# Silu by Tanh and root reciprocals by Newton steps on GpSimd, and the products of a slice ordered by columns, in a two-block fp32 transformer kernel

## The chip, the cores and the metric

The kernel runs on one core of one Trainium2 chip. The metric is the device time of one execution in microseconds (us). The time of a kernel is the median of several executions. Engines are called as in the profile: PE is TensorE's matmul, PEld its weight load, DVE is VectorE, ACT is ScalarE, POOL is GpSimd, SP is SyncE, which issues the weight loads from HBM.

## The reference

Two blocks follow each other on 256 tokens of width 2048, batch 1, all in float32.

The first block has two layers. Each layer modulates a root-mean-square norm (`x * rsqrt(mean(x^2) + 1e-6)`) with a shift and a scale that come from `silu(c) @ w_mod`, multiplies by `w_in` (2048 x 8192), and sends the result through a gated short convolution (`silu(z) * rmsnorm(b * conv(c * h))`) and through a bidirectional retention of 8 heads, whose output is normalised per head and multiplied by `silu(z)`. Both halves go through `w_out` (2048 x 2048), times a gate, into the residual. In layer 0 a context of 256 tokens takes the same way, so that 512 columns are worked on; layer 1 needs only keys and values of it.

The second block is a mixer with a state-space branch (causal convolution of width 4 with a bias and `silu`, a chunked scan, a gate `silu(z)`, a norm per group) and a dilated window attention branch with softmax, over `w_in_2` (2048 x 12320) and `w_out_2` (4096 x 2048), and then a squared-ReLU feed-forward net (2048 to 8192 to 2048). Each of the two is followed by a norm and added to the residual.

The new arithmetic rests on two identities: `silu(z) = (tanh(z/2) + 1) * z/2`, and Newton's step for `y = 1/sqrt(x)`, which is `y <- y * (1.5 - 0.5 * x * y * y)`.

## The kernel before

All products are float32 products on PE in the format fp32r, each made of three: an operand `w` is split into `wh` (what fp32r keeps) and `wl = w - wh`, the other operand likewise, and `wh*ah + wh*al + wl*ah` is summed in PSUM. Weights come from HBM through five buffers `raw` of 128 x 1024, by SP's queue. For each buffer ACT writes `wh` (an `ACTIVATE` of 128 x 1024, line L163) and DVE writes `wl` (a `TENSOR_TENSOR` of the same size, L166).

The program is written out in one order by a planner. `chunk` (from line 215) appends *jobs*. One job is one buffer of weights, usually two slices of 128 rows of the matrix (`kts`, a slice of k) for four column groups of 128 or one of 512. `run` (from line 365) goes through the jobs; for each it first emits the conversions of jobs up to four ahead (`AHEAD`), as far as a pair of `wh`/`wl` slots is free: three pairs always, and more where `room` lends a region of the activation arena `ar` to a stretch of jobs as `extra` slots. Then it emits the job's matmuls bank by bank (there are up to four PSUM banks `pm` to a job). After each bank comes an `event` (line 318): it emits what was put off by `later`, by one event or by `lag` of them. Once per job it takes a `step` (line 342) of the first *side*, a generator that holds the work beside the matmuls: `ret` (retention, one per two heads), `conv_fin`, `norms2`, `ssd`, `att`, `h2n_side`. A side whose `later` pieces are still waiting doesn't step. Every engine runs its own instructions in the order in which they were emitted, so a small matmul of a side stands between the big ones on PE, and PE waits there if its input is late.

Two kinds of products matter here. With `mmA` and `mmB` (lines 281 and 305) all matmuls of a bank have the same number of columns, 512 or 256. With `mmW` (line 288) a slice of k gives two matmuls: `wh` against 512 columns (`ah` and `al` side by side) and `wl` against the 256 columns of `ah`, added into the second half of the bank. In a job of two slices a bank's order is therefore 512, 256, 512, 256 columns, and the next bank goes on the same way. `mmW` serves the convolution columns of layer 1, the second half of layer 1's output product, most of the mixer's input product, the second half of its output product, and the feed-forward net's first product but for its first 1024 columns.

Norms are taken in one form, `rms_cols` (line 541): DVE scales the mean square and adds epsilon (L171), ACT takes `Sqrt` in place, DVE the `RECIPROCAL` (L544), on tiles of 128 x 2 or 128 x 4. Then PE spreads the column over the partitions (`spread`, line 557, four or eight small matmuls), and the normalising instructions read that. It is called once at the start (`prep_x`), twice in `norm1` (the context's and the tokens' norm ahead of layer 1), in `conv_fin` of both layers, twice in a row in `norms2`, in `norm3` and in `h2n_side`. `ret` (16 times), `ssd` (8 times) and the tail (`sums_out`, `scale_out`, twice) have their own `Sqrt`, put off by three events in `ret` and `ssd`, and `RECIPROCAL` (L852, L1462, L1846). `sqrt_table` makes ACT load the table of `Sqrt` ahead of `norm1` and `norm3`.

`Silu` is an `ACTIVATE` in six places: on `c` in `prelude`, on z in `evac_qz`, `conv_evac`, `conv_evac1` and `evac_z`, and after the convolution in `taps2`. `Exp` is used in `ret`, `ssd`, `att` and `dt_side`. A change between `Silu`, `Sqrt` and `Exp` puts an `ACT_TABLE_LOAD` in ACT's queue.

The feed-forward net starts right behind `norm3`: `h2_kt` (line 711) makes one slice of its input per job, with a chain of DVE (L174), POOL (L1715, a `TENSOR_TENSOR` add of 128 x 256), ACT and DVE. From the sixth job of this stretch on `room(u0 + 6, ...)` (line 1811) lends two more slots.

The tail: the last product's four banks are added (L166), squared and summed on ACT, multiplied by a weight on POOL (L1826); `sums_out`, `scale_out` and `store_out` (lines 1834 to 1854) scale 128 x 512 pieces on DVE (L174) and store them.

Of the kernel before, what the change touches and what calls it, by code (L numbers as in the profile page):

```python
# [10 lines left out]
OP = mybir.AluOpType  # L11
# [90 lines left out]
class Prog:  # L102
# [112 lines left out]
    def chunk(self, W, N, pieces, n, groups, items, mm, evac, pre=None, need=None, ord_=None, merge=False, fine=False, dense=False):  # L215
# [11 lines left out]
        for gi, kts in enumerate(groups):  # L227
            def pe(hi, lo, gi=gi, kts=kts):
# [8 lines left out]
                for bi, b in enumerate(order):  # L237
                    bank = st["banks"][b]
                    seq = [(h[:, ki], l[:, ki], kt) for h, l, ks in parts for ki, kt in enumerate(ks)]
                    for si, (h, l, kt) in enumerate(seq):  # L240
                        for ii, it in enumerate(items[b]):
                            todo = mm(it, kt, h, l)
                            for pi, (x, y, *at) in enumerate(todo):
                                o, n = at or (it["o"], it["n"])
                                self.mm(bank[:, o:o + n], x, y, start=gi == 0 and si == 0 and ii == 0 and pi == 0,
                                        stop=last and si == len(seq) - 1 and ii == len(items[b]) - 1 and pi == len(todo) - 1)
                        if (nb == 2 and si % 2 == 0 and len(kts) == 2) or (dense and last and si < len(seq) - 1):
                            self.event()
                    self.event((lambda: evac(b, bank)) if last else None)
                    for _ in range(places.count(bi)):  # L250
                        yield
# [196 lines left out]
    def startup(self):  # L448
# [15 lines left out]
        self.b1 = self.small(32)  # L464

# [9 lines left out]
    def prelude(self):  # L475
# [5 lines left out]
        self.act(self.csil, self.cv("c", 0, 32).rearrange("p (v k) -> p v k", v=2), AF.Silu)  # L481
# [3 lines left out]
        for l in range(2):  # L485
            self.ts(self.b1[:, l * 16:(l + 1) * 16], self.cv("b_mod", l * 48 + 16, 16), 1.0, op0=OP.add)
        self.spawn(self.prep_x())
# [53 lines left out]
    def rms_cols(self, out, ms, k):  # L541
        self.ts(out, ms, k, EPS, OP.mult, OP.add)
        self.act(out, out, AF.Sqrt)
        self.nc.vector.reciprocal(out, out)  # L544
# [8 lines left out]

    def sqrt_table(self):
        self.act(self.tcol, self.ones[:, 0:1], AF.Sqrt)
# [195 lines left out]
    def evac_qz(self, t, bank):  # L751
        self.act(self.R["q"][:, t], bank[:, 0:256])
        self.act(self.R["z"][:, t], bank[:, 256:512], AF.Silu)
        if t < 2:
            self.later(lambda: self.rope(self.R["q"][:, t], t))
# [20 lines left out]
    def ret(self, l, g):  # L776
# [6 lines left out]
        for hh in range(2):  # L783
# [64 lines left out]
            self.later(lambda: self.act(sd, sd, AF.Sqrt), lag=3)  # L848
            yield

            def normed():
                self.nc.vector.reciprocal(sd, sd)  # L852
# [15 lines left out]
    def conv_evac(self, l, fts):  # L868
# [14 lines left out]
        def evac(b, bank):  # L883
# [6 lines left out]
            elif b == 3:  # L890
                self.act(Z, bank, AF.Silu)
# [18 lines left out]
    def conv_evac1(self, ft):  # L910
# [7 lines left out]
        def evac(b, bank):  # L918
# [15 lines left out]
            elif b == 3:  # L934
                self.later(lambda: self.total(Z, two), lambda: self.act(Z, Z, AF.Silu))
# [36 lines left out]
    def layer0(self):  # L972
# [90 lines left out]
        pre[6] = self.sqrt_table  # L1063
# [173 lines left out]
    def norms2(self, part):  # L1237
# [25 lines left out]
        self.r12c = r12  # L1263
# [12 lines left out]
        self.tt(r12, r1, r2, OP.mult)  # L1276
        self.rb12 = self.ssq[:, 0:256]
# [58 lines left out]
    def taps2(self, U, dst, ft):  # L1336
        w = [self.cv("conv_w_2", k * 32 + ft) for k in range(4)]
        self.ts(dst, U[:, 0:256], w[0])
        for k in range(1, 4):
            self.stt(dst, U[:, k:k + 256], w[k], dst, OP.mult, OP.add)  # L1340
        self.later(lambda: self.act(dst, dst, AF.Silu, bias=self.cv("conv_b_2", ft)), lag=3)
# [56 lines left out]
    def ssd(self, r, gi):  # L1398
# [59 lines left out]
        self.later(lambda: self.act(ss, ss, AF.Sqrt), lag=3)  # L1458
        yield

        def scaled():
            self.nc.vector.reciprocal(ss, ss)  # L1462
# [80 lines left out]
    def mixer(self):  # L1543
# [76 lines left out]
        for r in range(4):  # L1620
# [3 lines left out]
            def evac_z(t, bank, r=r):  # L1624
                self.act(self.Z[:, t * 512:(t + 1) * 512], bank, AF.Silu, scale=self.r12c[:, t:t + 1])
# [57 lines left out]
        for c in range(2):  # L1683
            def evac(b, bank, c=c):
# [8 lines left out]
                else:  # L1693
# [3 lines left out]
                       pre={13: self.sqrt_table} if c else {}, merge=c == 1)  # L1697
# [52 lines left out]
    def mlp(self):  # L1750
# [35 lines left out]
        for half in range(2):  # L1786
# [18 lines left out]
            for c in range(2 - 2 * half, 8):  # L1805
# [4 lines left out]
                if c == 5:  # L1810
                    self.room(u0 + 6, len(self.jobs), 0, 1)
# [22 lines left out]
    def sums_out(self, t):  # L1834
# [7 lines left out]
        self.act(k, k, AF.Sqrt)  # L1842

    def scale_out(self, t):
        k = self.kk[:, t:t + 1]
        self.nc.vector.reciprocal(k, k)  # L1846
# [62 lines left out]
```

## Time and profile before

| what | value |
|---|---|
| median of 3 runs | 3184.23 us (3183.41 to 3187.32) |
| the profiled execution's own time | 3183.1 us |
| its span, first to last instruction | 3181.3 us |
| its mean granted clock of PE | 0.992 of 2.4 GHz |
| PE busy | 98% of the span, 16520 matmuls |
| DVE, ACT, POOL busy | 67%, 45%, 4% |
| HBM traffic | 178 GB/s over the span |

A busy PE is not PE at its peak: a matmul's recorded length overlaps the next one's, so the pace is read from the distance of starts. In a row of the timeline the first number is the start in us from the start of the span, the second how long the merged instructions took, then engine, source line, operation, what is written and read, shape, count, and in brackets the idle time of the engine ahead of it and what ended it. A line is often that of a helper (L163 `act`, L166 `tt`, L170 and L171 `ts`, L174 `stt`, L177 `mm`, L180 `tr`). The tile names are the program's: `pm` and `ps` are PSUM banks, `farena` and `small` hold intermediate values.

### The profile page before, as it was taken

The page shows a single profiled execution, that of the slowest core. Times are in us where ns is not written, and L with a number is a line of the kernel's source. Part 1 is how long each engine was busy: PE and PEld are TensorE (multiplying, and loading weights), DVE is VectorE, ACT ScalarE, POOL GpSimd, SP SyncE. Part 2 cuts the span into 40 slices and gives each one's busy share as a digit, 9 for nine tenths or more (in the row PEclk, how much of TensorE's full clock was granted, in tenths as well). Part 3 has the DMA queues.
Part 4 walks back from the last instruction along what each step waited for, and adds up shares of the span by engine and source line. Part 5 has one row for each costly group of instructions (what it writes and reads, how often), then busy time and mean ns, then how long its engine had stood idle before and what let it go on. Part 6 is the DMA issues. An engine that isn't in the chain of part 4 may idle for free.

```text
span 3181.3 us, 43430 instructions
## 1 busy us (share of the span) xinstructions
PE 3124.2 (98%) x16520; PEld 2673.0 (84%) x16520; DVE 2116.9 (67%) x3321; ACT 1445.0 (45%) x1930; POOL 120.5 (4%) x144
## 2 busy tenths in 40 slices
PE   7899999999999999999999999999999999999998
PEld 4688888888888988888999888888998888888886
DVE  8757677686677666674767877777744664456644
ACT  6633232232332354454554555555544554454542
POOL 4300000000000000000000000000000200000000
PEclk8999999999999999999999999999999999999999
DMA  8854545555455466664556656556654556666663
GB/s 290 273 186 135 169 139 152 149 155 164 149 165 159 137 189 186 198 212 126 195 190 203 187 164 179 165 172 181 219 184 143 184 171 197 192 200 191 192 197 129
DMA packets 413569, 569.91 MB, mean 179 GB/s; under 512 B 24272, under 2 KB 254288, under 8 KB 412208
## 3 DMA queue, kind: packets, MB, share of 16 engines
q1 hardware_dynamic: 409520, 543.90, 55.5%
q0 software_dynamic: 3696, 19.04, 2.0%
q10 hardware_dynamic: 144, 4.19, 0.3%
q8 instruction: 129, 2.11, 0.3%
q14 instruction: 80, 0.66, 0.1%
HBM read 556.53 MB, written 10.52 MB: 178 GB/s over the span
## 4 chain that ended last, share of the span: by engine, by line
PE 92%; DVE 3%; DMA 2%; ACT 1%; issue 1%; POOL 1%; SPq 0%; DVEq 0%; ACTq 0%; POOLq 0%
PE pm L177 86%; PE ps L177 4%; PE ps L180 1%; DMA raw<-in_w_mod 1%; DVE wl L166 1%; POOL farena L1715 1%; DVE ar L166 1%; DVE farena L174 1%; ACT ar L163 0%; PE pm L180 0%; ACT wh L163 0%; DVE farena L166 0%; DMA farena<-acsum 0%; ACT ps L163 0%; DMA farena<-in_x 0%
## 5 line engine op out<-in xcount | busy, mean ns | idle before, releaser
L177 PE MATMUL pm<-ar,wh 128*128 128x512 f32 (+1 forms) x3920 | 1182.8, 372 | 2.9 <-ACT ar L163 1.6
L166 DVE TENSOR_TENSOR wl<-raw,wh 128x1024 fp32r<-128x1024 f32 x608 | 749.9, 1237 | 593.2 <-ACT wh L163 585.5
L163 ACT ACTIVATE wh<-raw 128x1024 fp32r<-128x1024 f32 x608 | 639.6, 1057 | 977.6 <-PE pm L177 814.4
L177 PE MATMUL pm<-ar,wl 128*128 128x256 f32 (+1 forms) x2752 | 851.5, 309 | 0.0
L177 PE MATMUL pm<-ar,ar 128*128 128x512 f32 (+1 forms) x4488 | 839.9, 344 | 0.6 <-DVE ar L174 0.3
L177 PEld LDWEIGHTS pm<-ar,wh 128*128 128x128 f32 x3920 | 706.8, 190 | 128.5 <-DVE ar L174 2.2
L177 PEld LDWEIGHTS pm<-ar,ar 128*128 128x128 f32 x4488 | 704.4, 189 | 104.3 <-DVE ar L174 1.8
L177 PE MATMUL pm<-wh,ar 128*128 128x512 f32 x2448 | 771.1, 391 | 0.0
L177 PEld LDWEIGHTS pm<-ar,wl 128*128 128x128 f32 x2752 | 521.7, 190 | 28.9
L177 PEld LDWEIGHTS pm<-wh,ar 128*128 128x128 f32 x2448 | 459.7, 188 | 95.2
L177 PE MATMUL pm<-wl,ar 128*128 128x512 f32 x1224 | 476.8, 390 | 0.0
L166 DVE TENSOR_TENSOR ar<-raw,ar 128x1024 fp32r<-128x1024 f32 x289 | 355.7, 1240 | 181.9 <-ACT ar L163 174.4
L163 ACT ACTIVATE ar<-raw 128x1024 fp32r<-128x1024 f32 x289 | 300.2, 1052 | 218.0 <-PE pm L177 160.0
L174 DVE SCALAR_TENSOR_TENSOR farena<-raw,small,farena 128x512 f32<-128x512 f32 x420 | 307.6, 749 | 7.9
L177 PEld LDWEIGHTS pm<-wl,ar 128*128 128x128 f32 x1224 | 230.0, 188 | 46.6
L163 ACT ACTIVATE farena<-pm 128x512 f32<-128x512 f32 (+1 forms) x269 | 145.4, 556 | 147.0 <-PE pm L177 125.2
L166 DVE TENSOR_TENSOR farena<-farena 128x256 f32<-128x256 f32 (+2 forms) x308 | 150.1, 500 | 49.7 <-ACT farena L163 46.9
L177 PE MATMUL ps<-farena 128*128 128x128 f32 (+2 forms) x800 | 133.3, 309 | 4.3 <-ACT wh L163 1.6
L177 PEld LDWEIGHTS ps<-farena 128*128 128x128 f32 x800 | 111.4, 191 | 15.4 <-DVE farena L166 2.1
L163 ACT ACT_TABLE_LOAD x83 | 106.5, 1283 | 5.2 <-DMA farena<-acsum 3.1
L163 ACT ACTIVATE farena<-farena 128x512 f32<-128x512 f32 (+3 forms) x92 | 53.5, 591 | 89.8 <-DVE farena L166 56.8
L174 DVE SCALAR_TENSOR_TENSOR farena<-farena,cv 128x256 f32<-128x256 f32 (+1 forms) x160 | 82.8, 524 | 6.8 <-ACT farena L163 2.2
(143 smaller groups left out, 1269.3 us busy)
## 6 DMA issues: line engine op xcount, KB each, us to landing
raw<-in_w_in SPq DMA_DIRECT2D x641, 256.0 KB, 3.3
raw<-in_w_mod SPq DMA_DIRECT2D x192, 512.0 KB, 4.1
raw<-in_w_out SPq DMA_DIRECT2D x128, 512.0 KB, 4.6
raw<-in_w_in SPq DMA_DIRECT2D x128, 512.0 KB, 3.9
raw<-in_w_up SPq DMA_DIRECT2D x128, 512.0 KB, 3.8
raw<-in_w_down SPq DMA_DIRECT2D x128, 512.0 KB, 4.7
farena<-xspill POOLq DMA_DIRECT2D x6, 1024.0 KB, 5.1
xspill<-farena ACTq DMA_DIRECT2D x1, 4096.0 KB, 12.4
```

The source lines that it names most:

```text
L163: return self.nc.scalar.activation(out, in_, func, scale=scale, **kw)
L166: return self.nc.vector.tensor_tensor(out, a, b, op)
L174: return self.nc.vector.scalar_tensor_tensor(out, a, s, b, op0, op1, **kw)
L177: return self.nc.tensor.matmul(out, lhsT, rhs, start=start, stop=stop)
L180: return self.nc.tensor.transpose(out, in_, self.ident)
L1715: add.tensor_tensor(self.h2[:, kt], self.h2[:, kt], t, OP.add)
```

## The change

`chunk` collects all matmuls of a bank in a job; where the numbers of columns differ (`mmW`) they are sorted by them, falling in the job's first and third bank and in the chunk's first job, rising in the second and fourth. `Silu` becomes ACT's `Tanh` of half the value and a `scalar_tensor_tensor` on DVE that multiplies `tanh + 1` by the value (its half is in a weight that follows, or in the scale). `Sqrt` and `RECIPROCAL` become `rroot`: two integer `tensor_scalar` on DVE for the first guess and four Newton steps, 16 instructions on POOL, on a scratch tile of 128 x 8. In `ret` and `ssd` they are emitted at once and no longer three events later; in the tail they are emitted in `scale_out`. `sqrt_table` is gone. The convolution's bias goes into its first tap. In the feed-forward net's first half the two extra slots are lent ten jobs later.

```diff
-                    for si, (h, l, kt) in enumerate(seq):
-                        for ii, it in enumerate(items[b]):
-                            todo = mm(it, kt, h, l)
...
+                    ops, mixed = [], False
                     for si, (h, l, kt) in enumerate(seq):
+                        for it in items[b]:
+                            for x, y, *at in mm(it, kt, h, l):
+                                mixed |= bool(at)
+                                ops.append((x, y, *(at or (it["o"], it["n"])), si))
+                    if mixed:
+                        ops.sort(key=lambda op: op[3] if gi and bi % 2 else -op[3])
+                    for pi, (x, y, o, n, si) in enumerate(ops):
+                        self.mm(bank[:, o:o + n], x, y, start=gi == 0 and pi == 0, stop=last and pi == len(ops) - 1)
...
+        self.rr = self.small(8)
...
-        self.act(self.csil, self.cv("c", 0, 32).rearrange("p (v k) -> p v k", v=2), AF.Silu)
+        self.ts(self.cv("c", 0, 32), self.cv("c", 0, 32), 0.5)
+        self.act(self.csil, self.cv("c", 0, 32).rearrange("p (v k) -> p v k", v=2), AF.Tanh)
+        self.silu(self.csil, self.csil, self.cv("c", 0, 32).rearrange("p (v k) -> p v k", v=2))
...
+        for name, n in (("conv_norm_w", 32), ("conv_w_2", 160)):
+            self.ts(self.cv(name, 0, n), self.cv(name, 0, n), 0.5)
...
     def rms_cols(self, out, ms, k):
         self.ts(out, ms, k, EPS, OP.mult, OP.add)
-        self.act(out, out, AF.Sqrt)
-        self.nc.vector.reciprocal(out, out)
+        self.rroot(out)
+
+    def rroot(self, x):
+        n, g, I = x.shape[1], self.nc.gpsimd, mybir.dt.int32
+        y, a = self.rr[:, 0:n], self.rr[:, 4:4 + n]
+        self.ts(y.bitcast(I), x.bitcast(I), 1, op0=OP.arith_shift_right)
+        self.ts(y.bitcast(I), y.bitcast(I), -1, 0x5f3759df, OP.mult, OP.add)
+        for i in range(4):
+            g.tensor_tensor(a, y, y, OP.mult)
+            g.tensor_tensor(a, a, x, OP.mult)
+            g.tensor_scalar(a, a, -0.5, 1.5, op0=OP.mult, op1=OP.add)
+            g.tensor_tensor(x if i == 3 else y, a, y, OP.mult)
+
+    def silu(self, out, t, h):
+        self.stt(out, t, 1.0, h, OP.add, OP.mult)
...
-    def sqrt_table(self):
-        self.act(self.tcol, self.ones[:, 0:1], AF.Sqrt)
...
-        self.act(self.R["z"][:, t], bank[:, 256:512], AF.Silu)
+        z = self.R["z"][:, t]
+        self.act(z, bank[:, 256:512], AF.Tanh, scale=0.5)
+        self.later(lambda: self.silu(z, z, bank[:, 256:512]))
...
-            self.later(lambda: self.act(sd, sd, AF.Sqrt), lag=3)
+            self.rroot(sd)
             yield
             def normed():
-                self.nc.vector.reciprocal(sd, sd)
...
-                self.act(Z, bank, AF.Silu)
+                self.act(Z, bank, AF.Tanh, scale=0.5)
+                self.later(lambda: self.silu(Z, Z, bank))
...
-        pre[6] = self.sqrt_table
...
-        self.ts(dst, U[:, 0:256], w[0])
+        self.ts(dst, U[:, 0:256], w[0], self.cv("conv_b_2", ft), OP.mult, OP.add)
...
-        self.later(lambda: self.act(dst, dst, AF.Silu, bias=self.cv("conv_b_2", ft)), lag=3)
+        t = U[:, 0:256]
+        self.later(lambda: self.act(t, dst, AF.Tanh), lambda: self.silu(dst, t, dst), lag=3)
...
-        self.later(lambda: self.act(ss, ss, AF.Sqrt), lag=3)
+        self.rroot(ss)
...
-                self.act(self.Z[:, t * 512:(t + 1) * 512], bank, AF.Silu, scale=self.r12c[:, t:t + 1])
+                z, th = self.Z[:, t * 512:(t + 1) * 512], self.f(4096 + t * 512, 512)
+                self.act(z, bank, scale=self.h12c[:, t:t + 1])
+                self.act(th, bank, AF.Tanh, scale=self.h12c[:, t:t + 1])
+                self.later(lambda: self.silu(z, th, z))
...
-                       pre={13: self.sqrt_table} if c else {}, merge=c == 1)
+                       merge=c == 1)
...
-                    self.room(u0 + 6, len(self.jobs), 0, 1)
+                    self.room(u0 + (6 if half else 16), len(self.jobs), 0, 1)
...
-        self.act(k, k, AF.Sqrt)
     def scale_out(self, t):
         k = self.kk[:, t:t + 1]
-        self.nc.vector.reciprocal(k, k)
+        self.rroot(k)
         self.tt(k, k, self.q[:, t:t + 1], OP.mult)
```

## Rows read from the trace of the kernel before

**Rows 1.** The page's first part: busy time, share of the span and instructions of each engine.
```profile
PE 3124.2 (98%) x16520; PEld 2673.0 (84%) x16520; DVE 2116.9 (67%) x3321; ACT 1445.0 (45%) x1930; POOL 120.5 (4%) x144
```
**Rows 2.** Busy time by stretches, the start: us, busy time of each engine, clock, DMA share, GB/s.
```profile
0.00:157.00 157.00, 125.12 (x483) 89.51 (x483) 122.37 (x131) 102.77 (x140) 64.36 (x47) 0.90 0.85 285
```
**Rows 3.** Waits of PE from 157 to 2436 us: waited for, total us, times, longest.
```profile
PE ps L177 <- ACT wh L163: 1.6, 1, 1.6
PE ps L177 <- DVE farena L166: 1.5, 2, 1.2
PE ps L177 <- ACT ar L163: 1.3, 1, 1.3
```
**Rows 4.** Timeline of PE in the feed-forward net's first product, columns 512 and 256 in turn.
```profile
2574.00 5.81 PE L177 MATMUL pm<-ar,ar 128*128 128x512 f32 x32
2579.65 0.40 PE L177 MATMUL pm<-ar,wh 128*128 128x512 f32 x1
```
**Rows 5.** Chain that ended last: a stretch of 512 columns alone, and one of 256.
```profile
157.25 68.23 PE pm L177 x300
...
1037.51 28.80 PE pm L177 x240
```
**Rows 6.** The page's fifth part, ACT's table loads: count, busy us and mean ns, idle ahead.
```profile
L163 ACT ACT_TABLE_LOAD x83 | 106.5, 1283 | 5.2 <-DMA farena<-acsum 3.1
```
**Rows 7.** Timeline of `norm3`: scaled mean square to reciprocal.
```profile
2442.64 0.16 DVE L171 TENSOR_SCALAR small<-ps 128x2 f32<-128x2 f32 x1 [1.73 <-PE ps L177]
...
2443.07 0.17 DVE L544 RECIPROCAL small<-small 128x2 f32<-128x2 f32 x1 [0.27 <-ACT small L163]
```
**Rows 8.** Timeline of POOL in the mixer: its smallest instructions.
```profile
1688.36 0.21 POOL L1344 MEMSET farena<- 128x3 f32 x4
```
**Rows 9.** Timeline of POOL, start of the feed-forward net: additions of 128 x 256.
```profile
2447.95 0.72 POOL L1715 TENSOR_TENSOR farena<-farena 128x256 f32<-128x256 f32 x1 [194.61 <-ACT ar L163]
...
2466.49 1.82 POOL L1715 TENSOR_TENSOR farena<-farena 128x256 f32<-128x256 f32 x1 [1.53 <-DVE farena L174]
2469.85 1.82 POOL L1715 TENSOR_TENSOR farena<-farena 128x256 f32<-128x256 f32 x1 [1.54 <-DVE farena L174]
```
**Rows 10.** Timeline of the tail: POOL's last two products, DVE's first scaling.
```profile
3168.68 2.48 POOL L1826 TENSOR_TENSOR farena<-farena 128x512 f32<-128x512 f32 x2 [0.19 <-ACT farena L163]
...
3170.07 2.30 DVE L174 SCALAR_TENSOR_TENSOR farena<-farena,small 128x512 f32<-128x512 f32 x2
```
**Rows 11.** Timeline of `norm1`, twice: the reciprocal, and the spread on PE.
```profile
1068.02 0.17 DVE L544 RECIPROCAL small<-small 128x2 f32<-128x2 f32 x1 [0.27 <-ACT small L163]
...
1068.93 0.60 PE L177 MATMUL ps<-ci,small 128*128 128x128 f32 x4
...
1078.74 0.17 DVE L544 RECIPROCAL small<-small 128x2 f32<-128x2 f32 x1 [0.27 <-ACT small L163]
...
1080.66 0.61 PE L177 MATMUL ps<-ci,small 128*128 128x128 f32 x4
```
**Rows 12.** Timeline of `conv_fin` in layer 1: reciprocal, spread, DVE's next conversion.
```profile
1570.62 0.17 DVE L544 RECIPROCAL small<-small 128x2 f32<-128x2 f32 x1 [0.27 <-ACT small L163]
1571.18 0.60 PE L177 MATMUL ps<-ci,small 128*128 128x128 f32 x4
...
1571.57 1.23 DVE L166 TENSOR_TENSOR wl<-raw,wh 128x1024 fp32r<-128x1024 f32 x1 [0.78 <-ACT wh L163]
```
**Rows 13.** Timeline of `norms2`: the last product of both reciprocals, and the spread.
```profile
1672.12 0.16 DVE L166 TENSOR_TENSOR small<-small 128x2 f32<-128x2 f32 x1
...
1673.38 1.05 PE L177 MATMUL ps<-ci,small 128*128 128x128 f32 x8
```
**Rows 14.** Busy time by stretches behind `norm3`: us, busy times, clock, DMA share, GB/s.
```profile
2446.10:2452.40 6.30, 6.30 (x28) 6.07 (x29) 3.51 (x7) 1.70 (x3) 1.46 (x2) 0.50 0.00 1
```
**Rows 15.** Timeline of `ssd`: the scaling by the root, the transposes on PE.
```profile
1831.09 0.62 DVE L170 TENSOR_SCALAR farena<-farena,small 128x256 f32<-128x256 f32 x2
...
1835.01 0.60 PE L180 MATMUL ps<-ci,farena 128*128 128x128 f32 x4
```

More of the change, by code (lines that the diff above doesn't have):

```diff
@@ L239, in pe @@
                     seq = [(h[:, ki], l[:, ki], kt) for h, l, ks in parts for ki, kt in enumerate(ks)]
+                    ops, mixed = [], False
                     for si, (h, l, kt) in enumerate(seq):
-                        for ii, it in enumerate(items[b]):
-                            todo = mm(it, kt, h, l)
[L243 to L248, printed above, removed]
+                        for it in items[b]:
[6 more added lines that the diff above has]
+                        self.mm(bank[:, o:o + n], x, y, start=gi == 0 and pi == 0, stop=last and pi == len(ops) - 1)
+                        if not mixed and (pi == len(ops) - 1 or ops[pi + 1][4] != si):
+                            if (nb == 2 and si % 2 == 0 and len(kts) == 2) or (dense and last and si < len(seq) - 1):
+                                self.event()
                     self.event((lambda: evac(b, bank)) if last else None)
@@ L934, in evac @@
             elif b == 3:
-                self.later(lambda: self.total(Z, two), lambda: self.act(Z, Z, AF.Silu))
+                self.later(lambda: (self.total(Z, two), self.act(two[0], Z, AF.Tanh, scale=0.5)),
+                           lambda: self.silu(Z, two[0], Z))
             else:
@@ L1262, in norms2 @@
         r1, r2, r12 = c[:, 6:8], c[:, 2:4], c[:, 4:6]
-        self.r12c = r12
+        self.r12c, self.h12c = r12, self.small(2)
         def rows():
@@ L1276, in norms2 @@
         self.tt(r12, r1, r2, OP.mult)
+        self.ts(self.h12c, r12, 0.5)
         self.rb12 = self.ssq[:, 0:256]
@@ L1457, in ssd @@
         self.ts(ss, ss, 1.0 / 256, EPS, OP.mult, OP.add)
-        self.later(lambda: self.act(ss, ss, AF.Sqrt), lag=3)
+        self.rroot(ss)
         yield
         def scaled():
-            self.nc.vector.reciprocal(ss, ss)
             for c in range(2):
```

## The prediction

> **What bounds the kernel.** I read the page's engine shares first: PE is busy for 98% of the span [rows 1]. The busy times by stretches then show where it isn't: in the first 157 us, where the DMA engines are busy for 0.85 and bring 285 GB/s [rows 2]; at the norms ahead of a new product; and in the tail. The list of PE's waits shows that between 157 and 2436 us PE lost to ACT and DVE only 1.6 + 1.5 + 1.3 = 4.4 us in the three largest entries [rows 3]. So the time is PE's pace in the big products, plus a few serial chains in which PE stands. DVE at 67% and ACT at 45% are cover. Work taken off ACT is worth what PE waits for it; a microsecond put into a serial chain is paid in full.
>
> **The order of the products.** In a stretch that alternates 512 and 256 columns, 32 matmuls (16 pairs) lie between the starts 2574.00 and 2579.65, 0.353 us for a pair [rows 4]. A stretch of 512 columns alone takes 68.23 / 300 = 0.227 us each, one of 256 alone 28.80 / 240 = 0.120 [rows 5], together 0.347. Alternating costs 0.006 us per pair. The code has 2688 such pairs (layer 1: 512 + 128; mixer: 128 + 256 + 512 + 256; feed-forward: 384 + 512). Falling, rising, falling, rising leaves two runs of each width per job of eight pairs, the chunk's first job four, on average 2.25 of 8: 72% of the change of width goes. 2688 x 0.006 x 0.72 = 12 us gained. The bounds are 0 (the cost is not in the alternation) and 16 (all of it).
>
> **The table loads.** 83 loads of 1283 ns are 106.5 us of ACT [rows 6], nearly all hidden behind PE. What they can give back is part of the 4.4 us of waits above, at products of `ret` and `ssd` that wait for an `Exp` or a copy behind a load. I take 2.5, between 0 and 4.4. At the start one load disappears too, ahead of the first `Sqrt`; I count it with the startup. The `Tanh` forms of `Silu` add some 80 passes of 128 x 256 or 128 x 512 on DVE; at the 0.4 to 0.7 us of such passes that is about 45 us over 2100 us, covered by DVE's idle third. If that cover were gone, PE would wait for `wl`. A PSUM bank is held one event longer, and the next chunk's fifth bank covers that.
>
> **A root on POOL.** Before, from the start of the scaling to the end of the reciprocal, the chain took 2442.64 to 2443.24 us: 0.60, of which 0.44 come behind the scaling [rows 7]. Now two small DVE instructions (about 0.19 each from start to start, by the scaling's 0.16 and a hop), a hop to POOL, 16 dependent POOL instructions and a hop back take that place. The two guesses and hops cost about what the `Sqrt` and reciprocal did, so each root comes later by the time of the 16, which I call c. No row shows so small a POOL arithmetic. From below: four memsets of 3 columns in 0.21 us, 0.05 each, c = 0.8 [rows 8]. From above: an addition of 256 columns in 0.72 us, c = 11.5 [rows 9]. Two products of 512 columns take 2.48, 1.24 each [rows 10]; the line through 0.72 and 1.24 has 0.52 us for 256 columns and leaves 0.20 for none. The chain is of that kind of instruction, so I take 0.20 and **c = 3.2 us**, with 2.4 to 4.0 as its likely spread.
>
> The rows show a second thing: the same addition takes 1.82 us when DVE converts weights beside it, 1.1 more [rows 9]. The Trainium skill (SBUF — State Buffer, "Who interferes with whom") says why: a DVE instruction with two SBUF inputs and a POOL instruction that reads SBUF exclude each other for a whole instruction. By that rule the trace's 1.82 is a wait for one conversion of 1.23. Taken to its end for every one of the 16, it is the third rival below; in the sum it isn't used, because in nearly all the serial chains DVE itself stands waiting for the root and converts nothing.
>
> **Where the root is paid.**
> - Startup: the first spread comes c later, but nothing large waits for its result soon, DMA is the limit there and five raw buffers run on; a load of 1.28 goes. 0.5, between -1.3 and 4.4.
> - `conv_fin` of layer 0: its spread is emitted three events after the root, in jobs of twice the length of layer 1's; that covers c. 0.
> - `norm1`: the slack from reciprocal to spread was 1068.93 - 1068.19 = 0.74 and 1080.66 - 1078.91 = 1.75 [rows 11]. PE stands c - 0.74 and c - 1.75: 2.5 + 1.4 = 3.9.
> - `conv_fin` of layer 1: slack 0.39, and a conversion at 1571.57 falls into the chain, one collision [rows 12]: c - 0.39 + 1.0 = 3.8.
> - `norms2`: two roots in series with slack 1673.38 - 1672.28 = 1.1 [rows 13]: 2c - 1.1 = 5.3. Behind them in DVE's queue stand conversions; two jobs of weights cover these. PE stands idle long enough that its clock may fall as it did behind `norm3`, where 6.30 us ran at 0.50 of the clock, the 1.2 GHz level, after the idle time there [rows 14]: 3.1 us lost. I take half, 1.6.
> - `norm3`: PE, DVE and ACT all wait: c = 3.2. Its clock is down already.
> - Tail: the first `scale_out` queues on POOL behind the last product, which ends at 3168.68 + 2.48 = 3171.16, and DVE's scalings, which started at 3170.07 [rows 10], wait behind it: 1.1 + c, less about 0.6 as they no longer share the port with POOL. The second root starts behind the next two scalings, where before its `Sqrt` ran beside them: c + 0.4. Together 2c + 0.9 = 7.3.
> - `ret` (16) and `ssd` (8): the scaling by the root starts at 1831.09 and the transposes at 1835.01 [rows 15]. If DVE waits there for all of c, the scaling ends at 1831.09 + 3.2 + 0.6 = 1834.9, just in time. DVE stands meanwhile, with `wl` conversions queued behind it, and POOL's memsets and DMA issues (the convolution's border, the scan's sums) queue behind the 16. I take 1, between 0 and 6. `h2n_side` holds DVE once in the same way: 0, the `wl` ahead cover it.
>
> Sum: 0.5 + 3.9 + 3.8 + 6.9 + 3.2 + 7.3 + 1 = 26.6 us lost.
>
> **The lent slots.** From 2466 on the feed-forward's start runs at 3.36 us per job, the distance of POOL's additions [rows 9], where 24 matmuls of 0.120 need 2.88. The loss of 0.48 lasts eight jobs, 3.8 us, and it sets in when the extra slots let conversions run beside the additions. Lent ten jobs later, they do so for the last two or so. 3.0 gained, between 0 and 3.8.
>
> **Sum.** The profiled execution took 3183.1 us, 1.8 over its span, 1.1 under the median of 3184.23. 3183.1 - 12 - 2.5 - 3.0 + 26.6 = **3192 us**. It hangs on c: with 2.4 the paid chains sum to 20 and the time is 3186, with 4.0 it is 3199 and with `ret` and `ssd` then late 3203. The sum changes by about 8 us for each microsecond of c.
>
> **Rivals.**
> 1. *POOL's small instructions are cheap.* The memsets' 0.05 each speak for it [rows 8], the line through the additions against it. With c = 0.8 the chains cost 0 (startup), 0.1, 0.4, 0.5, 0.8 and 2.5 us, about 4, and the gains stand: 3183.1 - 17.5 + 4 = 3170, faster. The point that decides is c = 1.5. The Trainium skill (GPSIMD Engine Reference, "2.1 Instruction dispatch") has a rule for it: a core starts the next instruction as soon as its own share of the last is done. By that rule the 16, each on its own partitions, run closer than their durations, and the trace bears it out for independent memsets alone. Chance 0.22.
> 2. *The order of widths isn't worth 12 us*, as PE's starts in the alternating stretch are late for another reason, such as reading two tiles in turn. Then 3192 + 12 = 3204. The even 0.353 speaks against it. Chance 0.12.
> 3. *Collisions in every chain of the sides*: DVE is kept busy with conversions and each POOL instruction waits 1.1 us behind one; DVE then stands up to 16 x 1.1 us longer at the scaling of `ret` and `ssd`. That holds itself back, since a standing DVE doesn't collide, but 1 us more in 24 places is 3216. Chance 0.10.
> 4. *`Tanh` and `Exp` lie in different tables*, so that the loads stay: 3192 + 2.5 = 3195. No row shows `Tanh`. Chance 0.05.
>
> **The numbers.** My forecast, the sum with c from 1.5 to 4, has 0.51; it lies from 3176 to 3203. The first rival carries the range a little below that, the second lies at its upper end, so 3170 to 3207 leaves out the first rival's cheapest cases and the third. A measurement of this kernel tells 0.2%, 6.4 us, from no change: faster is under 3177.9, slower over 3190.6. Faster has the first rival and little more: 0.24. Within 0.2% lie the values of c from about 1.5 to 3: 0.28. Slower: 0.48.
>
> **What would show it.** In the changed kernel's trace: 35 groups of 16 POOL instructions with 0.15 to 0.25 us from start to start; PE waiting for POOL 2 to 4 us at `norm1`, `conv_fin` of layer 1 and `norm3`, 5 at `norms2`; the last store some 7 us later after PE's end than before; 0.348 us per pair in the feed-forward's first product; one table load; additions of 0.7 us at its start. The prediction is wrong if the 16 take under 1.5 us or over 5, if a pair still takes 0.353, or if PE waits for `wl` in the mixer.

## The result, and the profile after

The changed kernel takes 3309.59 us (median of 4 runs, 3306.95 to 3312.41) beside 3183.82 of the kernel before: ratio 1.0389, interval 1.0375 to 1.0403. At 3184 us that is +123.9 us, far above the range. Below, a time "over before" is always a run's ratio minus one, times 3184 us; the intervals of the ratios are 3 to 5 us to either side.

The page's first part of the changed kernel, and the granted clock from its second:

```profile
PE 3153.6 (95%) x16520; PEld 2693.9 (81%) x16520; DVE 2152.9 (65%) x3441; ACT 1335.9 (40%) x1819; POOL 255.6 (8%) x704
...
PEclk8999999999999999999999999999999999999998
```

Beside [rows 1], PE fell from 98% to 95% of a longer span; ACT lost 109 us of work and nothing came of it; POOL did 135 us more. The mean granted clock is 0.98 (0.992 before).

What PE waited for in the whole span: the waiting tile and line, what it waited for, total us, times, longest.

```profile
PE ps L180 <- DVE farena L170: 25.8, 8, 5.7
PE ps L177 <- POOL small L566: 22.3, 6, 5.4
PE ps L180 <- DVE farena L166: 18.1, 12, 2.6
...
PE ps L177 <- DVE small L166: 7.7, 1, 7.7
```

These are four families of roots. L170 is the scaling in `ssd`, eight times; L566 is the last Newton instruction ahead of the spreads at the start, in `norm1`, `conv_fin` and `norm3`; L166 is mostly the product behind `ret`'s scaling; the 7.7 is `norms2`. Against the 4.4 us in [rows 3] they make 74 us. From one `ssd` step, in order of time, all engines, with rows left out where marked (in brackets the idle time ahead and its end):

```profile
2209.14 0.17 DVE L171 TENSOR_SCALAR small<-small 128x2 f32<-128x2 f32 x1
...
2209.72 1.23 DVE L166 TENSOR_TENSOR wl<-raw,wh 128x1024 fp32r<-128x1024 f32 x1
2209.87 1.13 POOL L563 TENSOR_TENSOR small<-small 128x2 f32<-128x2 f32 x1 [29.22 <-DVE small L171]
...
2211.08 0.20 POOL L564 TENSOR_TENSOR small<-small 128x2 f32<-128x2 f32 x1
2211.37 0.19 POOL L565 TENSOR_SCALAR small<-small 128x2 f32<-128x2 f32 x1
...
2214.94 0.19 POOL L566 TENSOR_TENSOR small<-small 128x2 f32<-128x2 f32 x1
2215.07 0.20 POOL L1371 MEMSET farena<- 128x3 f32 x4
2215.17 0.61 DVE L170 TENSOR_SCALAR farena<-farena,small 128x256 f32<-128x256 f32 x2 [4.22 <-POOL farena L1371]
2215.57 1.16 PE L180 MATMUL ps<-ci,farena 128*128 128x128 f32 x4 [5.64 <-DVE farena L170]
```

The first POOL instruction lasts until DVE's conversion beside it is done, the others 0.19 each and 0.27 to 0.29 from start to start. DVE finishes the conversion, has the scaling next in its queue and stands for 4.22 us; PE stands for 5.64. From the first of the 16 to the end of the last (c) I find 4.3 us in the eight roots where DVE converts nothing, 5.2 to 7.2 in the other 27, and 5.38 in the mean of all 35.

The tables did what the change says: 83 loads [rows 6] became one.

```profile
L163 ACT ACT_TABLE_LOAD x1 | 1.3, 1283 | 0.7 <-PEq L1927 0.7
```

### The profile page after: what moved, and what is told of

It reads as the page before. It is cut to its first block, busy times and chain, and to the rows that moved or that the text cites. A ratio compares the mean times of both kernels' runs of the same rounds, so it can differ in the third digit from the quotient of the medians.

```text
span 3310.6 us, 43941 instructions
## 1 busy us (share of the span) xinstructions
PE 3153.6 (95%) x16520; PEld 2693.9 (81%) x16520; DVE 2152.9 (65%) x3441; ACT 1335.9 (40%) x1819; POOL 255.6 (8%) x704
## 5 line engine op out<-in xcount | busy, mean ns | idle before, releaser
L166 DVE TENSOR_TENSOR wl<-raw,wh 128x1024 fp32r<-128x1024 f32 x612 | 754.4, 1237 | 582.1 <-ACT wh L163 573.5
L177 PE MATMUL pm<-ar,wh 128*128 128x512 f32 (+1 forms) x3984 | 1091.9, 372 | 5.5 <-ACT farena L163 2.9
L177 PE MATMUL pm<-ar,ar 128*128 128x512 f32 (+2 forms) x4392 | 832.2, 347 | 0.5 <-DVE ar L166 0.5
L177 PEld LDWEIGHTS pm<-ar,ar 128*128 128x128 f32 (+1 forms) x4392 | 699.5, 191 | 101.0 <-DVE ar L166 1.1
L177 PEld LDWEIGHTS pm<-ar,wh 128*128 128x128 f32 x3984 | 692.7, 192 | 92.1 <-ACT farena L163 3.5
L177 PE MATMUL pm<-ar,wl 128*128 128x256 f32 (+1 forms) x2784 | 685.4, 312 | 0.0
L177 PEld LDWEIGHTS pm<-ar,wl 128*128 128x128 f32 x2784 | 484.3, 192 | 67.1
L166 DVE TENSOR_TENSOR ar<-raw,ar 128x1024 fp32r<-128x1024 f32 x285 | 350.6, 1240 | 176.3 <-ACT ar L163 169.2
L174 DVE SCALAR_TENSOR_TENSOR farena<-raw,small,farena 128x512 f32<-128x512 f32 x420 | 307.6, 749 | 7.9
L563 POOL TENSOR_TENSOR small<-small 128x2 f32<-128x2 f32 (+2 forms) x140 | 49.3, 352 | 1890.6 <-DVE small L171 1882.4
L166 DVE TENSOR_TENSOR farena<-farena 128x256 f32<-128x256 f32 (+2 forms) x308 | 149.8, 499 | 65.0 <-ACT farena L163 50.8
L163 ACT ACTIVATE farena<-farena 128x512 f32<-128x512 f32 (+3 forms) x124 | 67.2, 547 | 216.0 <-DVE farena L174 111.5
L180 PE MATMUL ps<-ci,farena 128*128 128x128 f32 x316 | 55.1, 293 | 58.1 <-DVE farena L170 25.8
```

What stands on the lines that cost most here:

```text
L163: return self.nc.scalar.activation(out, in_, func, scale=scale, **kw)
L166: return self.nc.vector.tensor_tensor(out, a, b, op)
L174: return self.nc.vector.scalar_tensor_tensor(out, a, s, b, op0, op1, **kw)
L177: return self.nc.tensor.matmul(out, lhsT, rhs, start=start, stop=stop)
L180: return self.nc.tensor.transpose(out, in_, self.ident)
L563: g.tensor_tensor(a, y, y, OP.mult)
```

## The experiments

The expectations speak of PE's *excess*: for each product the distance from its start to the next start beyond 0.227 us (512 columns), 0.120 (256) or 0.060 (128), summed over the stretch from 1 us ahead of a root's first POOL instruction to 10 us behind its last. It holds waits and slow clock alike.

| run | what it is | median us | ratio (interval) | over before |
|---|---|---|---|---|
| changed kernel | all parts | 3309.59 | 1.0389 (1.0375 to 1.0403) | +123.9 |
| e1_sqrt_back | roots by Sqrt again | 3190.26 | 1.0026 (1.0015 to 1.0037) | +8.3 |
| e2_lag4 | scaling three events later | 3367.18 | 1.0581 (1.0565 to 1.0597) | +185.0 |
| e3_two_steps | 8 POOL instructions | 3235.66 | 1.0166 (1.0149 to 1.0183) | +52.9 |
| e4_newton_alone | before + roots | 3301.10 | 1.0375 (1.0360 to 1.0391) | +119.4 |
| e5_sort_alone | before + order | 3179.01 | 0.9982 (0.9974 to 0.9991) | -5.7 |
| e6_sort_slots | before + order + slots | 3175.84 | 0.9973 (0.9963 to 0.9983) | -8.6 |
| e7_newton_on_dve | the 16 on DVE | 3274.36 | 1.0280 (1.0266 to 1.0294) | +89.2 |
| e8_root_a_step_early | a job between | 3282.93 | 1.0306 (1.0290 to 1.0322) | +97.4 |
| e9_newton_in_sides | Newton in `ret`, `ssd` | 3264.98 | 1.0255 (1.0241 to 1.0269) | +81.2 |
| e10_fill | PE kept busy in `ssd` | 3301.66 | 1.0371 (1.0356 to 1.0387) | +118.1 |
| e11_taps_silu | e1, one Silu back | 3182.20 | 0.9992 (0.9984 to 1.0001) | -2.5 |
| e12_one_step | 4 POOL instructions | 3208.26 | 1.0076 (1.0059 to 1.0093) | +24.2 |
| e13_early_and_memsets | e8, memsets on DVE | 3270.37 | 1.0270 (1.0253 to 1.0287) | +86.0 |

### Which part costs: the roots undone, and the roots alone

```diff
-        self.rroot(out)
+        self.act(out, out, AF.Sqrt)
+        self.nc.vector.reciprocal(out, out)
```

(in `rms_cols`, and in the same way in `ret`, `ssd` and the tail; the second run is the opposite, the kernel before with `rroot` put in.)

> The changed kernel with every root by ACT's Sqrt and DVE's reciprocal again, at their old places (the three events of delay in ret and ssd, the tail's Sqrt ahead of its scaling, the two early table loads). Tanh for Silu, the products ordered by columns and the late slots stay. Theory A (the loss is the roots on POOL: each is 16 dependent instructions of 0.27 to 0.28 us from start to start, 4.3 us in all and 5.2 to 7.2 with collisions, and PE's excess near the 35 roots sums to some 130 us): all of the loss goes, 3165 to 3186, with some 60 loads of the Sqrt and Exp tables back and POOL at 4% again. Theory B (the Tanh passes on DVE and the missing events of the ordered products cost a large part, PE waiting for wl): over 3210.

> The kernel before with the roots alone changed: Newton steps on POOL, emitted as in the changed kernel; Silu, the order of the products and the slots as before. Theory A: the whole loss is there, without the gains of the other parts: 3305 to 3330. Theory B: under 3280, as a part of the loss is in what is left out.

The roots by Sqrt take 115.6 us off (1.0389 - 1.0026); the roots alone put 119.4 on. Theory A holds, though both runs miss its ranges by 4 us, e4 downwards and e1 upwards: the rest of the change costs 8.3 us, where the prediction had a gain of 17.5. Two things are open: why the roots cost four times the sum, and which other part loses.

### How the cost goes with the length of the chain

```diff
-        for i in range(4):
+        for i in range(2):
```

(`range(1)` in the other run; the last step writes the result.)

> The changed kernel with two Newton steps for four, so 8 POOL instructions for 16 in each of the 35 roots (this changes the computation: the roots have fewer right digits). c is then 2.2 us and with one collision about 3.1. Theory A: PE's excess falls by about 2.2 us in some 28 places and by the time at half clock where the wait gets short, 60 to 95 us in all: 3215 to 3250. If the fixed parts (the hops between the engines, a collision each) made the loss and not the number of instructions: over 3275. Theory B: no change from 3309.

> The changed kernel with one Newton step, 4 POOL instructions in each root (this changes the computation: the roots have two or three right digits). The roots cost 119 us over Sqrt at a mean c of 5.4 us and 45 us at 3.1, a line of 32.5 us per microsecond that meets zero at 1.7. With c at 1.1 to 2.1 (with a collision in most), theory A (cover of about 1.7 us in nearly every place, and each microsecond over it paid in nearly every place): 3186 to 3200. If the hops between the engines and the two guesses cost beside c: 3205 to 3225, half of what two steps still lost.

The mean c is 1.93, 3.11 and 5.38 us with one, two and four steps, and the roots cost 15.9, 44.6 and 115.6 us over e1: 24 us for each microsecond between the first two, 31 between the others. With two steps theory A holds: the number of instructions is what is paid. It isn't paid in nearly all of the 35 places, though, as a slope of 31 seems to say. Between two and four steps PE's excess near the roots grows by 67 us and the tail by 4, together the 71, but seven places show under 0.5 us of excess in both runs: the last `ret` of layer 0, five of the eight in layer 1, where the code has one more step ahead of the transposes, and `h2n_side`. Several others pay up to 3.8 us for the 2.3 by which c grew. With one step 3208.26 lies in the second theory's range and not in A's: either the hops and the guesses cost some 16 us beside c, or the cover isn't 1.7 us everywhere and the places with less pay from the start. The traces speak for the second: with one step the excess is 2.3, 3.1 and 4.6 us in the fourth, sixth and eighth `ssd` step, where e1 has 0.5 each, while all eight places of `ret` in layer 0 are as in e1. How the rest of the 15.9 us divides isn't shown.

### Where it is paid, and what the queues do

```diff
-        self.later(lambda: self.act(sd, sd, AF.Sqrt), lag=3)
+        self.rroot(sd)
```

(e1 with this in `ret`, and the same in `ssd`.)

> The first run (roots by Sqrt, all else as changed) with Newton steps on POOL in ret and ssd alone, 24 of the 35 roots; the eleven roots of the start, the norms and the tail stay with Sqrt. All 35 cost 119 us over the first run's 3190. If the sides pay as PE's excess near their roots says (87 us less some 10 that were there before): 3260 to 3272. If most of it comes from the eleven serial norms (as the prediction had it, 25.6 of 26.6): under 3230.

The run lies in the first range: 72.9 us of the 115.6 are the 24 roots of the sides, 42.7 the eleven others. The kernel before already showed how little room the sides have. DVE's last work ahead of the transposes, and the transposes, once in `ret` and once in the sixth `ssd` step, the one shown above:

```profile
262.76 0.69 DVE L166 TENSOR_TENSOR farena<-farena 128x512 f32<-128x512 f32 x1
...
264.20 0.60 PE L180 MATMUL ps<-ci,farena 128*128 128x128 f32 x4
...
2110.29 0.62 DVE L170 TENSOR_SCALAR farena<-farena,small 128x256 f32<-128x256 f32 x2
...
2111.55 0.60 PE L180 MATMUL ps<-ci,farena 128*128 128x128 f32 x4
```

264.20 - 263.45 = 0.75 us and 2111.55 - 2110.91 = 0.64. The row on which the prediction rested [rows 15] has 3.3; in `ssd` only the first two steps have that, the other six 1.5 or 0.6. In layer 0's `ret` five of the eight places have 0.75, three 3.3.

Then two tries at hiding the root behind more work.

```diff
-            self.later(normed)
+            self.later(normed, lag=4)
```

> The changed kernel with only the emission moved: in ret and ssd the scaling by the root is put off by four events and no longer by one, which puts it about where it stood before; the roots stay on POOL. Theory A1 (in these 24 places it is the place of emission that costs: the scaling comes one event after the root, DVE stands at it for all of c and PE behind DVE): the 87 us of PE's excess near these roots go but for some 5 to 15, 3225 to 3240. Theory A2 (the sides are late as a whole by c, so that a later emission only moves the wait to the next matmul): 3295 to 3320. Theory B as in the first run: no change from 3309.

All three theories are wrong: 61 us slower. A side steps once per job, and a job has four events. With a delay of four the scaling is emitted just ahead of the step that emits its reader, PE's transposes, so it only lost its distance to them; and DVE had more to do beside the root. POOL's and DVE's timelines of that run, in `ret`:

```profile
322.40 1.14 POOL L563 TENSOR_TENSOR small<-small 128x4 f32<-128x4 f32 x1 [49.08 <-DVE small L171]
323.62 0.59 POOL L564 TENSOR_TENSOR small<-small 128x4 f32<-128x4 f32 x1
324.29 0.69 POOL L565 TENSOR_SCALAR small<-small 128x4 f32<-128x4 f32 x1
...
332.13 0.20 POOL L566 TENSOR_TENSOR small<-small 128x4 f32<-128x4 f32 x1
...
323.40 2.98 DVE L174 SCALAR_TENSOR_TENSOR farena<-raw,small,farena 128x512 f32<-128x512 f32 x4
```

While DVE does its four passes of 0.75 us, each POOL instruction ends with one of them: one per 0.7 us instead of 0.28, and c is 9.9 us. PE's wait for L166 went to 57.9 us in 17 places, of 6.0 at most.

```diff
             self.rroot(sd)
             yield
+            yield
```

(the same in `ssd`, so that a whole job lies between root and scaling.)

> The changed kernel with one more step of the side between the root and the scaling by it, in ret and ssd alone, so that one job more lies between them; the roots stay on POOL. Theory A (a root of 5.3 us is free where a job of 5.5 us or more of other work lies behind it, as long as the side isn't late at its end): the 87 us of PE's excess near these 24 roots shrink to 10 to 35, 3230 to 3265. Theory E (a DVE that goes on working only makes the chain longer by collisions, up to 10 us as in the run with the later scaling, and the sides, a step longer, are drained at their end): over 3290.

It took 26.5 us off, less than theory A and more than theory E said. The `ssd` roots answer as A expected (their excess falls from 44 to 16 us); those of `ret` don't. There DVE now stands for something else:

```profile
332.88 0.20 POOL L566 TENSOR_TENSOR small<-small 128x4 f32<-128x4 f32 x1
333.01 0.10 POOL L912 MEMSET farena<- 128x4 f32 x1
333.15 0.69 DVE L166 TENSOR_TENSOR farena<-pm,farena 128x512 f32<-128x512 f32 x1 [3.21 <-POOL farena L912]
```

The convolution's product needs a border that POOL zeroes, and that memset stands in POOL's queue behind the 16.

```diff
-                self.nc.gpsimd.memset(U[:, :, 0:258:257], 0.0)
+                self.nc.vector.memset(U[:, :, 0:258:257], 0.0)
```

(with the three like it, on top of the run before.)

> The run with one more step between root and scaling, and the four memsets of the convolutions' borders on DVE and no longer on POOL, where they stood in the queue behind the 16 Newton instructions. In that run the roots of ssd lost 28 us less than in the changed kernel, those of ret nothing less, and DVE stood 3.2 us at a convolution's product until the memset behind the root was done. Theory G (in ret it is POOL's queue that passes the root's time on): the 41 us of PE's excess near ret's 16 roots fall by 12 to 30: 3252 to 3272. If it is the root itself or a later stage of the sides: 3277 to 3290.

11.4 us less, at the slow end of theory G's range: the queue passes on a part. In layer 0's `ret` the excess goes from 29 to 23 us only; c is 8.9 to 10.0 there in five of the eight places, as it was in e2 at its worst. What is left I put down to that and haven't separated.

### POOL or DVE for the 16

```diff
-        n, g, I = x.shape[1], self.nc.gpsimd, mybir.dt.int32
+        n, g, I = x.shape[1], self.nc.vector, mybir.dt.int32
```

> The changed kernel with the 16 Newton instructions on DVE and no longer on POOL, at the same places. Two dependent DVE instructions of the first guess stand 0.21 us apart, so c is about 3.4 us, with no hop and no collision. Theory A (what counts is c): some 30 us are lost per microsecond of c, by the run of two steps (74 us for 2.2 to 2.8 us), so 3240 to 3265. If the engine as such or its port matters more than the length of the chain: under 3220. If DVE's own time is what fails (35 x 3.4 = 119 us more on an engine that PE waits for): over 3290.

c is 3.18 us (0.20 from start to start) and the roots cost 80.9 us, not the 45 of two steps on POOL with nearly the same c. So c isn't the whole delay. In all eight `ssd` steps the scaling starts 3.2 to 3.3 us after the second guess in e3 and 4.2 to 4.3 here: a conversion of 1.2 us, which ran beside POOL's chain there, comes between DVE's chain and the scaling here. It is still 35 us better than POOL with its longer c. Of the forecasts none fits; the time lies 9 us above the first.

### What the clock adds

```diff
+            if g > 1:
+                both, ah = self.wide(1, 3, 0)
+                for _ in range(14):
+                    self.mm(ps[1], ah[:, 0:128], both)
```

(in `turned` of `ssd`, ahead of the transposes.)

> The changed kernel with 14 more products of 512 columns (3.2 us) on PE ahead of the transposes in the last six of the eight ssd steps, into a PSUM bank that is free there; they compute nothing that is used. PE waits there 2.3 to 5.8 us for the root, and its excess after that is 2.3 to 2.9 us more in each, 15 us in all, with the granted clock at 0.68 to 0.86 over ten microseconds. Theory F (that part is the clock at its lower level after PE stood): the clock stays up in the places with the short waits and falls less in the others, and the six places lose 3 to 13 us less: 3297 to 3307, although PE has more to do. If the excess is late work and not the clock: 3310 to 3325.

The stretch of the `ssd` step shown above, in the changed kernel: us, busy time of each engine, granted clock, DMA share, GB/s.

```profile
2210.00:2220.00 10.00, 4.43 (x16) 3.87 (x17) 4.43 (x7) 1.90 (x3) 4.03 (x20) 0.68 0.36 104
```

The same step with the added products, first in the same view, then in PE's timeline:

```profile
2203.00:2213.00 10.00, 7.58 (x41) 6.12 (x40) 5.18 (x8) 1.79 (x3) 4.16 (x20) 1.00 0.34 96
```

```profile
2203.17 3.38 PE L177 MATMUL ps<-ar 128*128 128x512 f32 x14
2208.97 0.81 PE L180 MATMUL ps<-ci,farena 128*128 128x128 f32 x4 [2.42 <-DVE farena L170]
```

The clock stays at 1.00 although the wait is still 2.42 us long behind the products. In the changed kernel it stood at 0.50, the 1.2 GHz level, from 2213.6 to 2220.5, in this step, and for 3.4 or 6.8 us in each of the six; in e10 it falls in none of them. PE's excess in the six places is 28.7 us less (40.4 in the changed kernel, 11.7 here), while the products take 84 x 0.227 = 19.1 us, so 9.6 us are gained there. The run lies in theory F's range and its median gives 5.8 us back, but that is about as much as the intervals of the two ratios; the places show it better than the times. So a part of a long wait's price is the 1.2 GHz level that comes with it. Over the span the granted clock falls short of full speed by 0.02 x 3310 = 66 us, before by 0.008 x 3181 = 25; a part of the difference lies in the waits themselves, where it costs nothing.

### The other parts

```diff
+                    if mixed:
+                        ops.sort(key=lambda op: op[3] if gi and bi % 2 else -op[3])
```

> The kernel before with the products of a bank ordered by columns, and nothing else. Theory C1 (the change of width costs, and nothing takes the place of what is saved): 6 to 10 us less, 3172 to 3178; the excess of PE's starts that lies in steps under 0.1 us fell by 8 us from the kernel before to the first run, which has the order. Theory C2 (in jobs of ordered products the event between two slices is gone, so that pieces put off by events come later, and PE's waits at the sides eat the gain): 3180 to 3190.

```diff
-                    self.room(u0 + 6, len(self.jobs), 0, 1)
+                    self.room(u0 + (6 if half else 16), len(self.jobs), 0, 1)
```

> The run before this one with the two extra slots lent ten jobs later in the feed-forward net's first half as well, and so the first run without Tanh. If the additions on POOL are slowed by the conversions that the early slots let run: 3 to 4 us under the run before. If not: the same. What this run lies under the first run is the price of the Tanh form: theory D1, 10 to 20 us, as the first run came out 7.6 over the kernel before although it has the order and the slots; theory D2 (Tanh is free and the order is what costs): under 3 us.

The order gains 5.7 us, just short of C1's 6 to 10. PE's timeline in the feed-forward net's first product, with the order:

```profile
2565.73 1.09 PE L177 MATMUL pm<-ar,wh 128*128 128x512 f32 x4
2566.66 0.63 PE L177 MATMUL pm<-ar,wl 128*128 128x256 f32 x4
2567.13 1.09 PE L177 MATMUL pm<-ar,wh 128*128 128x512 f32 x4
```

Four pairs take 2567.13 - 2565.73 = 1.40 us, 0.350 each; 0.353 in alternation [rows 4]. The slots add 2.9 us, less than the intervals of the two ratios can tell apart, but their place is plain. POOL's additions at the net's start, with the early slots (e5) and with the late ones (e6):

```profile
2468.25 1.82 POOL L1720 TENSOR_TENSOR farena<-farena 128x256 f32<-128x256 f32 x1 [1.53 <-DVE farena L174]
2471.60 1.82 POOL L1720 TENSOR_TENSOR farena<-farena 128x256 f32<-128x256 f32 x1 [1.53 <-DVE farena L174]
```

```profile
2468.66 0.74 POOL L1720 TENSOR_TENSOR farena<-farena 128x256 f32<-128x256 f32 x1 [2.14 <-DVE farena L174]
2471.55 0.74 POOL L1720 TENSOR_TENSOR farena<-farena 128x256 f32<-128x256 f32 x1 [2.14 <-DVE farena L174]
```

A job takes 2.89 us now, PE's own pace, and no longer 3.35. This run is the fastest of all, 0.27% (0.17 to 0.37) under the kernel before.

e1 differs from it by the Tanh form alone, tables included (83 loads before, 56 in e1): 16.9 us (1.0026 - 0.9973), theory D1.

```diff
-        t = U[:, 0:256]
-        self.later(lambda: self.act(t, dst, AF.Tanh), lambda: self.silu(dst, t, dst), lag=3)
+        self.later(lambda: self.act(dst, dst, AF.Silu, bias=self.cv("conv_b_2", ft)), lag=3)
```

> The first run with Silu from ACT's table again behind the mixer's convolution (its bias in the ACTIVATE), so that Tanh stays on c and in the four gates z. The first run lies 15 us of span over the run with the order and the slots, and 9 of it come in the mixer's first 120 us. Theory D3 (it is the DVE pass of 128 x 256 behind each Tanh of the convolution, which stands in DVE's queue behind a conversion while PE's transposes wait for it): 3179 to 3184, for all that Silu, Tanh and Exp change tables again. Theory D4 (the price is in the gates, or the tables that return cost as much): 3186 to 3196.

Theory D3 holds: 10.8 of the 16.9 us are the Silu behind the mixer's convolution. One of the places, in e1 (DVE, then PE):

```profile
1811.10 1.52 DVE L174 SCALAR_TENSOR_TENSOR farena<-farena,cv 128x256 f32<-128x256 f32 x3
1812.54 1.22 DVE L166 TENSOR_TENSOR wl<-raw,wh 128x1024 fp32r<-128x1024 f32 x1
1813.67 0.42 DVE L174 SCALAR_TENSOR_TENSOR farena<-farena 128x256 f32<-128x256 f32 x1
...
1814.15 0.48 PE L180 MATMUL ps<-ci,farena 128*128 128x128 f32 x1 [3.42 <-DVE farena L174]
```

The new pass of 0.42 us stands behind a conversion of 1.22, and PE waits 3.42 us for it. In e11 it waits 0.72 us in this place, for ACT. There are four such waits for L174 in e1, 5.3 us in all, and none in e11; how the rest of the 10.8 comes about isn't shown. The other 6 us lie in the five remaining places of Silu and in the tables; they weren't split.

## Why the prediction was wrong

The two sums, part by part:

| step | predicted | measured | by |
|---|---|---|---|
| order of the products | -12 | -5.7 | e5 |
| lent slots | -3.0 | -2.9 | e6 - e5 |
| Tanh and tables (83 loads to 56) | -2.5 | +16.9 | e1 - e6 |
| roots, at a c of 3.1 to 3.2 | +26.6 | +44.6 | e3 - e1 |
| roots, c from there to 5.4 | 0 | +71.0 | changed - e3 |
| sum | +9.1 | +123.9 | |

- **The length of a root.** "I take 0.20 and c = 3.2 us." The duration was right (0.19 to 0.20), but the row that I extrapolated has no dependent neighbour: from start to start it is 0.27 to 0.29, 4.3 us for 16. Then the sentence "in nearly all the serial chains DVE itself stands waiting for the root and converts nothing" holds in eight of the eleven roots of the start, the norms and the tail, and in none of the 24 in `ret` and `ssd`. In those DVE has one conversion or more ahead of the scaling, and c is 0.9 to 2.9 us longer by the collisions. The mean over all, 4.3 + 1.1, is the 5.4 measured, over the 5 that the prediction named as a sign that it is wrong. The third rival had this mechanism, with a chance of 0.10, but its 1 us more in 24 places makes 3216: it took the places to have the slack of the sum.
- **The places that pay.** "`ret` (16) and `ssd` (8) ... I take 1, between 0 and 6": 72.9 us. I read one slack, 3.3 us in the first `ssd` step [rows 15], and took it for 24 places, while the trace had 0.6 and 0.75 in others, shown above. So the slope is 24 to 31 us per microsecond of c and not 8. Neither error alone makes the result: by the prediction's own slope a c longer by 2.2 us costs 18 us more, and the wrong places cost 18 more at a c of 3.1 (44.6 - 26.6). The other 53 of the 89 us by which the roots were off come of both together. The eleven others cost 42.7, predicted 25.6 at the shorter c. Of `norm1`, `norms2` and the tail the form of the terms was right, their c too short: with 4.3 they give 3.6, 2.6, 7.5 and 9.5 us; PE stood 3.7, 2.4 and 7.7, and the span ends 9.0 us later after PE's last product. `conv_fin` of layer 0 was put at 0, as covered, and PE stood 2.0 us there; the start was put at 0.5, and PE stood 5.4 us for its first spread; how much of that is lost, with the weights still on their way, isn't shown. DVE's two waits in the tail:

```profile
3295.67 0.16 DVE L166 TENSOR_TENSOR small<-small 128x1 f32<-128x1 f32 x1 [5.83 <-POOL small L566]
...
3303.76 0.16 DVE L166 TENSOR_TENSOR small<-small 128x1 f32<-128x1 f32 x1 [4.46 <-POOL small L566]
```

- **The clock** was counted once, at `norms2` (1.6 us). It falls at the long waits in the sides as well, to 0.50 for 6.8 us in the `ssd` step shown, and where products filled such waits it fell in none of the six places.
- **Tanh.** "Covered by DVE's idle third" looked at `wl` alone, the wrong reader. Behind the convolution the pass isn't too much work for DVE, it is a link more in a chain with PE at its end; for the other 6 us that is not shown.
- **The tables** went as forecast, 83 to one, so the fourth rival is out. What this is worth can only be bounded: order, slots and Tanh cost 8.3 us where 56 loads stay (e1), and 123.9 - 119.4 = 4.5 us where e4's 46 become one; the 4 us between them lie inside the intervals.
- **The order**: right in kind, half in size. Four products of 512 columns in a run take 0.93 us (2565.73 to 2566.66), not 4 x 0.227 = 0.91, so 0.003 us per pair are saved and not 0.004; the second rival (nothing) is out.
- **The slots**: as forecast, by the mechanism named.
- The first rival (cheap POOL instructions) was the one that I gave most after the forecast; 0.05 us in [rows 8] are for memsets that don't depend on each other, and say nothing of a chain, whose instructions start further apart (0.27 to 0.29) than they last.
- A reading: the three entries of [rows 3] aren't the three largest in that stretch; PE also waited 1.7 us, once, for DVE's L174. Nothing in the sum hangs on it.

The Trainium skill's rule (SBUF — State Buffer, "Who interferes with whom") that the prediction set aside is what e2 shows: a POOL instruction that reads SBUF ends with the DVE pass of two inputs beside it, 0.58 to 0.71 us instead of 0.20.

## What to carry to other kernels

A step that many places share has as many slacks: list the distance from its last instruction to its reader for every place, and price the change place by place, not by one of them. Price a serial chain by start-to-start distances of *dependent* instructions, and add what stands behind it on its engine, what another engine does beside it (DVE's conversions here), and the slow clock that comes with a long wait. A little work taken off an engine that PE doesn't wait for (ACT here) pays for nothing that is put into a chain at whose end PE stands.

## What the runs showed of the hardware

- Dependent POOL instructions on 128 x 1 to 128 x 4: 0.19 us each, 0.27 to 0.29 from start to start; on DVE 0.16 and 0.20. Beside a DVE pass of two inputs the same POOL instruction ended with that pass, after up to 1.2 us.
- `Tanh` and `Exp` ran from one table: a single load in the changed kernel.
- 3.2 us of products ahead of a wait of 2.4 us kept the granted clock at 1.00, where without them it was 0.68 over ten microseconds, 0.50 for 6.8 of them.
- DVE's conversion beside a chain on POOL lengthened the chain; with the chain on DVE it came behind it, and the reader was 1.1 us later for nearly the same c (3.1 and 3.2 us).
